# A two-layer network in fast block products: the second product in 26 block products of three slices instead of 20 of four

## Chip, core and metric

The kernel runs on one core of one Trainium2 chip. The metric is the device time of one execution in microseconds (us). The time of the kernel before is the median of three runs; one further execution was profiled.

## What is computed

```python
# x [8192 x 768] (16 x 512 rows), w1 [768 x 3072], b1 [3072], w2 [3072 x 768], all float32
y = np.matmul(x, w1) + b1
y = np.maximum(y, 0)
return np.matmul(y, w2).astype(np.float32)
```

## The kernel before, in words

**Halves and iterations.** The 3072 hidden columns are cut into two halves (c = 0 and 1), the 8192 rows into 8 blocks of 1024. The 16 iterations go through the 8 blocks with the first half of w1 and w2 resident in on-chip memory, and then through the 8 blocks with the second. In the first eight iterations the output rows are stored, in the last eight they are added to what is stored, by accumulating DMAs of GpSimd's queue (POOL).

**Fast block products.** Both products are cut into blocks and computed with fewer block products than the plain way, in the manner of Strassen: sums of blocks of the left operand are multiplied by sums of blocks of the right one, and the results are combined. Tables say how. X_SUMS and W1_SUMS give the block sums of the first product, FIRST_U and FIRST_V which sum goes into which of its 20 products, FIRST_OPS the operations that combine results; Y_SUMS, W2_SUMS, SECOND_U, SECOND_V and SECOND_OPS are the same for the second. The block sums of x and y are made anew in each iteration, on VectorE (add_x_sums, L682; add_y_sums, L908); those of w1 and w2 once for each half (L699, L723). X_FUSE and Y_FUSE name sums that are done two at once, as one instruction over two blocks ("two-wide").

**First stage of an iteration** (add_first, L917): two groups of 20 products of 6 matmuls each (L935, 128x256), 240 matmuls. The results in PSUM, TensorE's accumulator memory, are combined by ScalarE (L965, L969) and VectorE (L972, L975, L981), and the last operation of a chain adds the bias, applies the relu and writes y as float16. In iteration 0 a plain product (L845) stands in its place.

**Second stage** (add_second, L1034): 20 products, each of a 256-row by 512-column block of y (sums of y in the slots that ys gives) and a block of w2 (512 by 384). A product is 8 matmuls: four slices s of the hidden columns, summed in PSUM, times two groups j of 128 rows (L1056, 128x384).

**Chains, operations and places.** SECOND_CHAINS lists, for each of seven chains, products ('m', n) and operations ('t', n) in turn. A chain owns a pair of PSUM banks while it lasts; there are four pairs. An operation takes the pair's running result after the product ahead of it: a 'sum' is kept in on-chip memory (a place of tile s), a 'seed' is written into another chain's bank pair as that chain's start value, an 'out' is a block of the output (a place of tile o), which a DMA stores. An operation with a kept sum to add runs on VectorE (L1071), one without on ScalarE (L1068). A product that goes on in a pair waits for the operation that reads the pair before it, and the one that starts on a seed waits for the seed. So an operation lies on a loop: end of one product, operation, start of a later product on the same pair.

**Order.** SECOND_ORDER gives the order of the 20 products in an iteration. A planner in the program (Graph.run) takes all tasks with a duration each, and the order of the products as given, and writes out one fixed order for each engine; take (L300) picks places of s, o and PSUM. At run time there are only these fixed queues and semaphores between engines. SP issues the plain stores, weight loads of the second half and transposing loads of x, POOL the loads of x and the accumulating stores.

**Special iterations.** In the iterations of APART (7) the kept sum and the product's own part of an output are stored apart, the second one accumulating. In the last iteration add_priors loads the rows that the first half stored, VectorE adds them and the outputs go by plain stores; the last output is stored in two halves by two queues (L1087).

Of the kernel before, what the change touches and what calls it, by code (L numbers as in the profile page):

```python
# [9 lines left out]
FP32 = mybir.dt.float32  # L10
FP16 = mybir.dt.float16
# [19 lines left out]
X_SUMS = ((20, 4, 3, -1), (15, 4, 1, -1), (21, 7, 1, -1), (12, 0, 4, -1), (10, 5, 1, -1), (13, 0,  # L31
    6, -1), (11, 2, 6, -1), (22, 6, 7, -1), (16, 0, 1, -1), (17, 6, 1, -1), (23, 6, 3, -1), (14,
    7, 3, -1), (18, 3, 2, -1), (19, 4, 2, -1), (9, 4, 5, -1), (8, 5, 3, -1))
FIRST_U = (22, 13, 17, 8, 16, 19, 6, 14, 1, 4, 21, 18, 10, 3, 11, 9, 12, 20, 23, 15)
W1_SUMS = ((6, 2, 5, 1), (8, 6, 4, -1), (17, 1, 8, -1), (7, 0, 1, 1), (10, 8, 7, -1), (16, 3, 10,
    -1), (9, 6, 3, -1), (11, 4, 5, -1), (12, 9, 0, -1), (14, 7, 9, -1), (15, 3, 5, -1), (13, 7, 2,
    -1))
FIRST_V = (15, 0, 9, 3, 2, 0, 12, 4, 6, 17, 3, 13, 4, 16, 1, 11, 1, 10, 14, 8)
FIRST_OPS = {
    0: (0, 1, 18, 1, 'out', 0, None),  # L40
    1: (4, 1, 17, 1, 'out', 1, None),
    2: (3, 1, 19, 1, 'out', 2, None),
    3: (6, 1, 15, 1, 'out', 3, None),
    4: (7, 1, None, None, 'out', 4, (1.0, 1.0, -1.0)),
    5: (7, 1, 15, 1, 'out', 5, None),
    6: (2, 1, None, None, 'out', 6, None),
    7: (5, 1, 17, 1, 'out', 7, None),
    8: (5, 1, 19, 1, 'out', 8, None),
    9: (1, 1, 18, 1, 'out', 9, None),
    10: (6, 1, None, None, 'out', 10, (0.0, 1.0, 0.0)),  # L50
    11: (1, 1, None, None, 'out', 11, (0.0, 0.0, 1.0)),
    12: (0, 1, None, None, 'seed', 1, None),
    13: (6, 1, None, None, 'seed', 7, (-1.0, 0.0, 1.0)),
    14: (4, 1, None, None, 'seed', 5, None),
    15: (8, -1, None, None, 'sum', None, (1.0, 0.0, 0.0)),
    16: (8, -1, 20, 1, 'seed', 2, None),
    17: (8, 1, 19, 1, 'sum', None, (0.0, 1.0, -1.0)),
    18: (6, -1, 20, 1, 'sum', None, None),
    19: (0, 1, None, None, 'sum', None, (0.0, 0.0, 1.0)),
    20: (6, 1, None, None, 'sum', None, (1.0, 0.0, 0.0)),  # L60
}
FIRST_CHAINS = ((('m', 8), ('t', 19), ('m', 2), ('t', 12), ('m', 1), ('t', 0)), (('m', 10), ('t',
# [4 lines left out]
FIRST_SEEDS = (None, 12, 16, None, None, 14, None, 13, None)  # L67
FIRST_ORDER = (19, 8, 9, 24, 28, 13, 17, 4, 22, 29, 12, 3, 16, 5, 15, 33, 39, 37, 6, 32, 25, 36,
    23, 2, 18, 30, 26, 14, 1, 38, 35, 7, 10, 34, 21, 20, 27, 11, 0, 31)
SWITCH_ORDER = (19, 8, 9, 24, 28, 13, 17, 4, 22, 29, 12, 3, 16, 5, 15, 33, 39, 37, 6, 32, 25, 36,  # L70
    23, 2, 18, 30, 26, 14, 1, 38, 35, 7, 10, 34, 21, 20, 27, 11, 0, 31)

Y_SUMS = ((13, 8, 7, 1), (16, 5, 3, 1), (12, 2, 1, 1), (20, 7, 10, 1), (15, 4, 12, -1), (24, 2, 0,
    1), (19, 10, 13, 1), (23, 15, 9, -1), (26, 23, 3, -1), (14, 0, 6, -1), (17, 2, 14, 1), (18, 9,
    16, 1), (27, 14, 15, -1), (22, 17, 20, 1), (21, 18, 19, 1), (25, 11, 21, 1))
SECOND_U = (4, 11, 5, 25, 8, 13, 15, 12, 27, 19, 17, 6, 22, 24, 16, 2, 26, 18, 10, 9)
W2_SUMS = ((7, 2, 1, -1), (13, 7, 5, -1), (6, 2, 0, -1), (10, 5, 6, -1), (8, 5, 4, -1), (9, 3, 8,
    1), (12, 7, 9, -1), (15, 8, 7, -1), (11, 9, 6, -1), (14, 1, 11, 1), (16, 3, 10, 1), (17, 5, 2,
    -1))
SECOND_V = (1, 5, 6, 17, 7, 1, 11, 4, 14, 13, 12, 0, 15, 3, 0, 9, 16, 10, 4, 3)  # L80
W2_NEG = (3,)
SECOND_OPS = {
    0: (0, 1, 11, 1, 'out', 2, None),
    1: (2, 1, 9, 1, 'out', 3, None),
    2: (1, 1, 11, 1, 'out', 0, None),
    3: (2, 1, None, None, 'out', 1, None),
    4: (1, 1, 8, 1, 'out', 4, None),
    5: (3, -1, 8, 1, 'out', 5, None),
    6: (0, -1, 9, 1, 'out', 6, None),
    7: (3, 1, None, None, 'out', 7, None),  # L90
    8: (1, -1, 13, 1, 'sum', None, None),
    9: (0, 1, 10, 1, 'sum', None, None),
    10: (4, 1, 16, 1, 'sum', None, None),
    11: (5, 1, None, None, 'sum', None, None),
    12: (5, -1, None, None, 'seed', 0, None),
    13: (6, 1, None, None, 'sum', None, None),
    14: (5, 1, 16, -1, 'seed', 2, None),
    15: (1, -1, None, None, 'seed', 5, None),
    16: (1, -1, None, None, 'sum', None, None),
    17: (3, -1, 19, 1, 'seed', 1, None),  # L100
    18: (4, -1, None, None, 'seed', 3, None),
    19: (6, 1, None, None, 'sum', None, None),
}
SECOND_CHAINS = ((('m', 2), ('t', 9), ('m', 14), ('t', 0), ('m', 3), ('t', 6)), (('m', 9), ('t',
# [4 lines left out]
SECOND_SEEDS = (12, 17, 14, 18, None, 15, None)  # L109
SECOND_ORDER = (19, 5, 1, 4, 9, 18, 13, 17, 10, 15, 12, 11, 6, 7, 2, 0, 14, 8, 16, 3)  # L110
LAST_ORDER = (19, 5, 1, 4, 9, 18, 13, 17, 10, 15, 12, 11, 6, 7, 2, 0, 14, 8, 16, 3)

X_FUSE = (6, 8, 10, 12)
Y_FUSE = (5, 10, 13)
# [100 lines left out]

class Reg:
# [14 lines left out]
class Graph:  # L231
# [9 lines left out]
    def __init__(self, banks=8, sums=12, outs=4):  # L241
        self.tasks = []
        self.writer, self.readers = {}, {}
        self.npe = 0
        self.places = {"ps": [[0.0, 0] for _ in range(banks)],
                       "s": [[0.0, 0] for _ in range(sums)], "o": [[0.0, 0] for _ in range(outs)]}
# [53 lines left out]
    def take(self, reg, start, but=()):  # L300
# [22 lines left out]
        step = reg.n if reg.kind == "s" else 1  # L323
        for i in range(0, len(p) - reg.n + 1, step):
            f = max(p[k][0] for k in range(i, i + reg.n))
            if f < 1e8 and (best is None or f < best[0]):
                best = (f, list(range(i, i + reg.n)))
        return best

    def run(self, begin=0.0, lookahead=0.2, ahead=5):  # L330
# [5 lines left out]
        far = at + 50.0  # L336
# [128 lines left out]
APART = (7,)  # L465

W2_WHOLE = (4, 0)
# [3 lines left out]
class Fast:  # L471
# [6 lines left out]
    def __init__(self, nc, xf, w1, b1, w2, of):  # L478
# [8 lines left out]
        self.g = Graph()  # L487
        nw1, self.nsum = self.NCH * 12, self.NCH * 24
# [4 lines left out]
    def place_all(self):  # L493
        self.xs = place({r * 2 + k: 2 * r + k for r in range(4) for k in range(2)}, X_SUMS,
                        FIRST_U, range(8, 20))
        self.ys = place({r * 3 + h: r * 3 + h for r in range(4) for h in range(3)}, Y_SUMS,
                        SECOND_U, range(12, 20))
        self.w1s = place({k * 3 + h: 2 * h + k for k in range(2) for h in range(3)}, W1_SUMS,
                         FIRST_V, range(6, 16))
        self.w2s = [place({n * 3 + h: 2 * h + n for n in range(2) for h in range(3)}, W2_SUMS,  # L500
                          SECOND_V, range(6, 16))]
# [4 lines left out]
        self.w2s.append(place(dict(enumerate(freed[:6])), W2_SUMS, SECOND_V, freed[6:]))  # L506

    def open(self, ctx, tc):
# [9 lines left out]
        self.v2 = one.tile([P, 16, 4, self.NH], FP16, name="v2")  # L518
        self.y = one.tile([P, 20, 4 * self.QM], FP16, name="y")
        self.x = one.tile([P, 20, 3, self.QM], FP16, name="x")  # L520
        self.xn = one.tile([P, 8, self.K], FP16, name="xn")
        self.s = one.tile([P, 12, 256], FP32, name="s")
        self.o = one.tile([P, 4, self.N], FP32, name="o")
        self.ps = pool("ps", 1, space=PSUM).tile([P, 8, 512], FP32, name="ps")
        self.w1dram = dram.tile([P, self.NG, 6, 3, 2 * P], FP16, name="w1d")
        self.w2dram = dram.tile([P, 6, 4, self.NH], FP16, name="w2d")
# [3 lines left out]
    def constants(self):  # L530
        nc = self.nc
        nw1, nw2, nx, nb = self.NCH * 12, self.NCH * 12, self.M // P, self.H // P
# [32 lines left out]
    def load_w2(self, to, c, h, s):  # L565
        h0 = (12 * c + 4 * h + s) * P
        self.nc.gpsimd.dma_start(out=to[:, 2 * h:2 * h + 2, s, :],
                                 in_=self.w2[h0:h0 + P, :].rearrange("p (a n) -> p a n", a=2))
# [12 lines left out]
    def prologue(self):  # L581
        nc = self.nc
        for s in range(4):
            (nc.sync, nc.scalar)[s % 2].dma_start(out=self.o[:, s],
# [7 lines left out]
        self.load_strip(self.v1, 0, 1, 0)  # L592
# [753 lines left out]
```

## Time and profile before

| what | value |
|---|---|
| time, median of 3 runs | 865.16 us (863.69 to 865.88) |
| profiled execution, its own time | 863.6 us |
| its span (first to last instruction) | 862.1 us |
| granted clock of TensorE | 0.997 of full |
| busy: PE 850.1, DVE 699.0, ACT 475.1, POOL 125.2 us | 99, 81, 55, 15% of the span |
| moved by DMA | 117.50 MB |

PE is TensorE's matmul part, PEld its weight load, which runs beside it, DVE is VectorE, ACT ScalarE, POOL GpSimd, SP SyncE. In the rows, L1056 is line 1056 of the program; out<-in are tiles; the time in brackets is the engine's idle time ahead of the instruction and what ended it. A matmul's end is modelled: it stands until its results are through, some 0.16 us after the next matmul has begun, so that matmuls overlap in the rows, and their starts are what the pace is read from.

### The profile page before, as it was taken

The numbers are of one execution on the slowest core, as the hardware profiler recorded it, in microseconds if no ns is written. First come the engines' busy times: TensorE is split into PE (matmuls) and PEld (weight loads), VectorE is DVE, ScalarE is ACT, GpSimd is POOL, SyncE is SP. The second block draws the span as 40 slices with busy tenths as digits, with TensorE's granted clock in tenths as the row PEclk, the third lists the DMA queues.
The fourth block names the chain that finished last, engine by engine and source line by source line (L and its number), as shares of the span: only waits on it lengthen the run. The fifth ranks groups of instructions, "written<-read, shape, count | busy, mean of one in ns | idle before, by whom it ended". The sixth has DMA issues, their size and how long they took to land. (4 is left out here: it accounts for less than half of the span.)

```text
span 862.1 us, 16228 instructions
## 1 busy us (share of the span) xinstructions
PE 850.1 (99%) x6445; PEld 631.4 (73%) x6445; DVE 699.0 (81%) x1043; ACT 475.1 (55%) x945; POOL 125.2 (15%) x143
## 2 busy tenths in 40 slices
PE   8999999999999999999999999999999999999996
PEld 7568778686786868768587686867868687686873
DVE  5789887968778797887989879687786978779786
ACT  5736747566574763835658265745738336253350
POOL 5200010201001010000121303113040220402200
PEclk9999999999999999999999999999999999999998
DMA  9993494865839465480896947698786787954743
GB/s 213 198 193 100 86 258 91 162 146 93 208 74 196 113 105 156 74 220 22 277 188 85 199 69 134 121 136 130 111 127 106 121 125 124 138 89 61 128 144 129
DMA packets 161347, 117.50 MB, mean 136 GB/s; under 512 B 93148, under 2 KB 159732, under 8 KB 161012
## 3 DMA queue, kind: packets, MB, share of 16 engines
q0 software_dynamic: 48128, 56.63, 42.2%
q1 hardware_dynamic: 112672, 58.81, 27.8%
q8 instruction: 51, 0.84, 0.4%
q10 hardware_dynamic: 468, 1.00, 0.3%
q14 instruction: 28, 0.23, 0.1%
HBM read 73.94 MB, written 57.41 MB: 152 GB/s over the span
## 5 line engine op out<-in xcount | busy, mean ns | idle before, releaser
L1056 PE MATMUL ps<-v,y 128*128 128x384 f16 x2560 | 418.9, 326 | 0.1
L935 PE MATMUL ps<-x,v 128*128 128x256 f16 x3600 | 396.1, 273 | 0.9 <-DVE o L1071 0.5
L935 PEld LDWEIGHTS <-v 128*128 128x128 f16 x3600 | 352.2, 98 | 44.0 <-issue 1.7
L1056 PEld LDWEIGHTS <-y 128*128 128x128 f16 x2560 | 250.5, 98 | 164.5 <-issue 0.6
L972 DVE CUSTOM_DVE_ANT_0 y<-ps,s 128x512 f16<-128x512 f32 x240 | 161.4, 688 | 63.5 <-PE ps L935 45.7
L908 DVE TENSOR_TENSOR y<-y 128x1024 f16<-128x1024 f16 (+2 forms) x227 | 165.5, 754 | 4.9 <-ACT y L854 2.2
L969 ACT ACTIVATE s<-ps,bt 128x256 f32<-128x256 f32 x180 | 73.9, 472 | 115.7 <-PE ps L935 114.2
L682 DVE TENSOR_TENSOR x<-x 128x768 f16<-128x768 f16 (+1 forms) x168 | 109.7, 684 | 0.5
L1101 POOL DMA_DIRECT2D out_dram<-o x62 | 74.4, 1275 | 178.2 <-DMA out_dram<-s 60.8
L1068 ACT ACTIVATE ps<-ps 128x768 f32<-128x768 f32 x48 | 38.2, 795 | 110.0 <-PE ps L1056 94.2
L579 POOL DMA_DIRECT2D xn<-in_x_dram x30 | 22.9, 763 | 491.1 <-ACT xn L641 352.4
L1068 ACT ACTIVATE s<-ps 128x768 f32<-128x768 f32 x64 | 51.8, 811 | 61.0 <-PE ps L1056 60.1
L969 ACT ACTIVATE y<-ps,bt 128x256 f16<-128x256 f32 x180 | 73.5, 472 | 15.7 <-PE ps L935 13.9
L1071 DVE TENSOR_TENSOR o<-ps,s 128x768 f32<-128x768 f32 x56 | 52.9, 954 | 8.9 <-PE ps L1056 4.7
L641 ACT ACTIVATE xn<-xn 128x768 f16<-128x768 f16 x64 | 53.5, 838 | 3.9 <-DMA x<-xn 2.5
L1071 DVE TENSOR_TENSOR s<-ps,s 128x768 f32<-128x768 f32 x32 | 30.6, 956 | 11.4 <-PE ps L1056 11.1
L981 DVE TENSOR_TENSOR s<-s,ps 128x512 f32<-128x512 f32 x30 | 20.5, 684 | 19.0 <-PE ps L935 19.0
L969 ACT ACTIVATE ps<-ps,bt 128x256 f32<-128x256 f32 x60 | 26.9, 448 | 16.3 <-PE ps L935 8.7
L1068 ACT ACTIVATE o<-ps 128x768 f32<-128x768 f32 x36 | 29.0, 809 | 12.1 <-PE ps L1056 12.0
L965 ACT ACTIVATE ps<-ps 128x512 f32<-128x512 f32 x60 | 34.9, 582 | 0.9 <-DVE y L972 0.2
L845 PE MATMUL ps<-x,v 128*128 128x256 f16 (+1 forms) x216 | 31.9, 308 | 0.9 <-DMA v<-in_w_dram 0.6
L1071 DVE TENSOR_TENSOR o<-s,ps 128x768 f32<-128x768 f32 x28 | 26.6, 949 | 7.2 <-DMA out_dram<-o 6.1
(61 smaller groups left out, 353.7 us busy)
## 6 DMA issues: line engine op xcount, KB each, us to landing
out_dram<-o SPq DMA_DIRECT2D x65, 384.0 KB, 6.4
out_dram<-o POOLq DMA_DIRECT2D x62, 384.0 KB, 6.9
xn<-in_x_dram POOLq DMA_DIRECT2D x28, 768.0 KB, 8.3
x<-out_dram SPq DMA_DIRECT2D x8, 384.0 KB, 3.3
v<-in_w_dram POOLq DMA_DIRECT2D x6, 384.0 KB, 9.1
v<-in_w_dram POOLq DMA_DIRECT2D x12, 192.0 KB, 10.0
w1d<-in_w_dram POOLq DMA_DIRECT2D x6, 384.0 KB, 15.8
w2d<-in_w_dram POOLq DMA_DIRECT2D x12, 192.0 KB, 13.7
```

What stands on the lines that cost most here:

```text
L641: self.nc.scalar.activation(out=self.xn[:, s, :], in_=self.xn[:, s, :], func=ACTF.Square, accum_out=self.stat[:, self.stat_at["x"] + i:][: ...
L682: self.nc.vector.tensor_tensor(out=self.two(x, out), in0=self.two(x, in0), in1=self.two(x, in1), op=ALU.add if sign > 0 else ALU.subtract)
L845: nc.tensor.matmul(self.ps[:, ps.at[0], cols], lhsT=self.v1[:, gi, 2 * h + k2, k, j * P:(j + 1) * P], rhs=rhs, start=(k2 == 0 and k == 0), ...
L908: self.nc.vector.tensor_tensor(out=self.two(y, out), in0=self.two(y, in0), in1=self.two(y, in1), op=ALU.add if sign > 0 else ALU.subtract)
L935: nc.tensor.matmul(self.ps[:, at, j * self.QM:(j + 1) * self.QM], lhsT=self.v1[:, gi, self.w1s[FIRST_V[p]], k, j * P:(j + 1) * P], rhs=sel ...
L965: nc.scalar.activation(out=out, in_=ps, scale=float(a), func=func if kind == "out" else ACTF.Copy)
L969: nc.scalar.activation(out=out[:, halves[j]], in_=ps[:, halves[j]], func=func, scale=float(a), bias=beta(j))
L972: nc.vector._custom_dve(TENSOR_ADD_SAT, out=out, in0=ps, in1=s, s0=F_MAX, s1=0.0)
L1056: nc.tensor.matmul(self.ps[:, bank[ch].at[j], 0:NH], lhsT=self.y[:, self.ys[SECOND_U[p]], m0:m0 + P], rhs=self.v2[:, slot[SECOND_V[p]], s, :],
L1068: nc.scalar.activation(out=out, in_=ps, func=ACTF.Copy, scale=float(a))
L1071: engine.tensor_tensor(out=out, in0=in0, in1=in1, op=ALU.add if a == b else ALU.subtract)
L1101: nc.gpsimd.dma_start(out=rows, in_=out, accum_op=ALU.add)
```

## The change

The second product is cut another way. A block of y has 256 rows and 384 hidden columns (three slices h, was four slices s), a block of w2 384 by 384. A 4 by 4 arrangement of y blocks times a 4 by 2 arrangement of w2 blocks takes 26 products of 6 matmuls (was a 4 by 3 times 3 by 2 arrangement in 20 products of 8). With it come:

- 28 sums of y blocks (was 16), 18 of w2 blocks (was 12), new chains (eight), operations (26) and order. Five pairs of y sums are two-wide (was three), two of x (was four).
- y has 23 slots of 768, fewer than the 16 blocks and 28 sums. A new function, place_between, puts a sum into the slot of one that is no longer needed, and says after which product that may be. add_y_sums is called ahead of every product and adds the sums whose slot the product before has freed; before, all sums stood ahead of the first product.
- Kept sums and outputs share one tile s of eight places, each of 768 float32; before they had s (12 places of 256) and o (four of 768). An operation that uses a kept sum for the last time writes over it.
- The first product's tables are new as well (again 20 products in two groups); its outputs go to two y slots each.
- Output operation 6 (SPLIT) stores its kept sum and its product's part apart in every iteration, 7 and 8 are the iterations that do so for all (APART, was 7).
- In the last iteration only the outputs of LAST_DIRECT take loaded priors; the others are accumulated by POOL.
- w1 sums are made for each group alone (was both at once), w2 sums whole (1152 elements). All six loads of w1 stand ahead of those of w2 at the start; for the second half w1 is loaded in 12 DMAs (was 2), w2 in 8 (was 6).

The core of the diff:

```diff
-SECOND_ORDER = (19, 5, 1, 4, 9, 18, 13, 17, 10, 15, 12, 11, 6, 7, 2, 0, 14, 8, 16, 3)
+SECOND_CHAINS = ((('m', 5), ('t', 2)), (('m', 24), ('t', 0)), (('m', 13), ('t', 24), ('m', 4),
+    ('t', 23), ('m', 12), ('t', 18), ('m', 1), ('t', 17), ('m', 23), ('t', 9), ('m', 16), ('t',
+    4), ('m', 9), ('t', 5)), (('m', 10), ('t', 22), ('m', 18), ('t', 20), ('m', 0), ('t', 15),
+    ('m', 14), ('t', 6)), (('m', 17), ('t', 21), ('m', 8), ('t', 19), ('m', 3), ('t', 16), ('m',
+    19), ('t', 14), ('m', 7), ('t', 8), ('m', 6), ('t', 3), ('m', 20), ('t', 1)), (('m', 2), ('t',
+    13), ('m', 21), ('t', 12), ('m', 25), ('t', 7)), (('m', 11), ('t', 11), ('m', 22), ('t', 10)),
+    (('m', 15), ('t', 25)))
+SECOND_SEEDS = (8, 10, None, 23, 24, 18, 13, None)
+SECOND_ORDER = (13, 15, 4, 17, 10, 8, 18, 12, 3, 0, 1, 2, 14, 23, 19, 21, 11, 25, 7, 16, 22, 5, 6,
+    9, 24, 20)
+LAST_DIRECT = (0, 1, 2, 3, 5)
-X_FUSE = (6, 8, 10, 12)
-Y_FUSE = (5, 10, 13)
+X_FUSE = (0, 2)
+Y_FUSE = (7, 9, 13, 18, 26)
+S_SLOTS, Y_SLOTS = 8, 23
...
+def place_between(order, sums, used, raw, slots, fused):
+    slot, live, free = {n: n for n in range(raw)}, set(range(raw)), list(range(raw, slots))
+    last = {used[p]: n for n, p in enumerate(order)}
+    since, at = [], -1
+    for n, (o, _, _, _) in enumerate(sums):
+        later = {v for s in sums[n + 1:] for v in s[1:3]}
+        old = sorted(live - later, key=lambda v: (last.get(v, -1), v))
+        for v in old:
+            if v not in last:
+                live.discard(v)
+                free.append(slot[v])
+        if not free:
+            v = [v for v in old if v in last][0]
+            at = max(at, last[v])
+            live.discard(v)
+            free.append(slot[v])
+        slot[o] = free.pop(0)
+        live.add(o)
+        since.append(at)
...
-APART = (7,)
+SPLIT = (6,)
+APART = (7, 8)
...
-    def add_y_sums(self, groups=(0, 1)):
+    def add_y_sums(self, order, done):
+        n, since = 0, self.y_from[order]
+        for out, in0, in1, sign in self.sums_of(Y_SUMS, self.ys[order], Y_FUSE):
+            at, n = n, n + len(out)
+            if since[at] != done - 1:
+                continue
...
-            sj = [(s, j) for s in range(4) for j in range(2)]
+            hj = [(h, j) for h in range(3) for j in range(2)]
...
-                                 lhsT=self.y[:, self.ys[SECOND_U[p]], m0:m0 + P],
-                                 rhs=self.v2[:, slot[SECOND_V[p]], s, :],
-                                 start=(start and s == 0), stop=(s == 3), skip_group_check=True)
+                                 lhsT=self.y[:, ys[SECOND_U[p]], m0:m0 + P],
+                                 rhs=self.v2[:, slot[SECOND_V[p]], h, :],
+                                 start=(start and h == 0), stop=(h == 2), skip_group_check=True)
...
             if kind == "m":
+                self.add_y_sums(order, done)
+                done += 1
...
                 if what == "sum":
-                    dest = kept[n] = Reg("s", 3)
+                    dest = kept[n] = Reg("s") if u is None or u in uses else kept[u]
```

More of the change, by code (lines that the diff above doesn't have):

```diff
@@ L68 @@
[L68 to L75, printed above, removed]
@@ L213, in place @@
     return slot
+def place_between(order, sums, used, raw, slots, fused):
[17 more added lines that the diff above has]
+        since.append(at)
+    for n in fused:
+        since[n] = since[n + 1]
+    made = {s[0]: since[n] for n, s in enumerate(sums)}
+    for n, p in enumerate(order):
+        assert made.get(used[p], -1) < n, p
+    return slot, since
 class Reg:
@@ L763, in add_stats @@
                 for i in range(6) if first and (i in FIRST_V) == kept]
-        todo += [lambda i=i: self.add_stat_w2(c, i, after) for i in range(6)
+        todo += [lambda i=i: self.add_stat_w2(c, i, after) for i in range(8)
                  if second and (i in SECOND_V) == kept]
@@ L1037, in add_second @@
         final = it == self.NIT - 1
-        apart = it in APART
+        apart = {t for t in SECOND_OPS if (t in SPLIT or it in APART)
+                 and SECOND_OPS[t][2] is not None and not (final and t in LAST_DIRECT)}
         order = LAST_ORDER if final else SECOND_ORDER
-        slot = self.w2s[c]
-        bank, kept = {}, {}
+        slot, ys = self.w2s[c], self.ys[order]
+        bank, kept, done = {}, {}, 0
+        uses = [SECOND_OPS[t][2] for t in SECOND_OPS]
         NH, QM = self.NH, self.QM
@@ L1076, in operation @@
             ps = pair(bank[ch])
[L1077 to L1087 removed]
+            out = pair(dest) if kind == "seed" else sum_of(dest)
+            if kind == "out" and final and t in LAST_DIRECT:
+                if t in folds:
+                    combine(nc.scalar, out, ps, a, None, None)
                 else:
@@ L1118, in add_second @@
                     bank[ch] = Reg("ps", 2, leaves=1)
-                u, w = self.ys[SECOND_U[n]], slot[SECOND_V[n]]
-                self.g.add("PE", 1301, lambda p=n, ch=ch, start=start: product(p, ch, start),
-                           reads=self.y_keys(u, 0) + self.y_keys(u, 1) +
-                           [("w2", w, s) for s in range(4)] + ([] if start else [bank[ch]]),
-                           writes=[bank[ch]])
+                t = SECOND_CHAINS[ch][-1][1]
+                if final and t in LAST_FOLD and t in LAST_DIRECT and not start and SECOND_CHAINS[ch][-2] == ("m", n):
+                    fold(t)
+                    folds.add(t)
+                u, w = ys[SECOND_U[n]], slot[SECOND_V[n]]
+                self.g.add("PE", 976, lambda p=n, ch=ch, start=start: product(p, ch, start),
+                           reads=self.y_keys(u) + [("w2", w, h) for h in range(3)] +
+                           ([] if start else [bank[ch]]), writes=[bank[ch]])
                 continue
@@ L1205, in plan @@
         self.presets()
-        self.hold = [g.held(Reg("o"), [s]) for s in range(4)]
+        self.hold = [g.held(Reg("s"), [s]) for s in range(4)]
         self.first_block()
```

469 lines of the change are left out of this document (252 added, 217 removed), and 16 rows, old and new, of tables (FIRST_CHAINS, SECOND_CHAINS, Y_SUMS).

## The prediction

> **What bounds the kernel now.** I read the page's busy times first, then the waits of TensorE, then two stages in the middle of the run, then single instructions at their edges. Columns of the first rows: busy us (share), instructions; below, the groups have busy us, mean ns of one | idle before.
>
> ```profile
> span 862.1 us, 16228 instructions
> PE 850.1 (99%) x6445; PEld 631.4 (73%) x6445; DVE 699.0 (81%) x1043; ACT 475.1 (55%) x945; POOL 125.2 (15%) x143
> ...
> L1056 PE MATMUL ps<-v,y 128*128 128x384 f16 x2560 | 418.9, 326 | 0.1
> L935 PE MATMUL ps<-x,v 128*128 128x256 f16 x3600 | 396.1, 273 | 0.9 <-DVE o L1071 0.5
> ```
>
> TensorE is busy for 99% of the span, and 815 us of that are two lines. The list of TensorE's waits has only single short ones; its longest and its only one on a result of the second product:
>
> ```profile
> PE ps L601 <- DVE ones L542: 1.3, 1, 1.3
> ...
> PE ps L935 <- DVE o L1071: 0.5, 1, 0.5
> ```
>
> One second stage (304.25 to 330.25) and the first stage behind it, with busy time of each engine, granted clock, DMA share and GB/s:
>
> ```profile
> 304.25:330.25 26.00, 26.00 (x162) 15.65 (x160) 23.64 (x31) 12.48 (x23) 2.88 (x4) 1.00 0.76 162
> 330.25:356.45 26.20, 26.20 (x242) 23.48 (x240) 18.55 (x30) 16.05 (x38) 0.00 (x0) 1.00 0.43 97
> sum 52.20, PE 52.20 PEld 39.14 DVE 42.19 ACT 28.53 POOL 2.88; mean PE 26.10 PEld 19.57 DVE 21.10 ACT 14.27 POOL 1.44
> ```
>
> TensorE fills both stages at the full clock. VectorE has 10 of 52.2 us free, so TensorE's stream sets the time, and it stays so only while every eviction comes back before TensorE needs the bank pair. How near that is, single instructions show (start, length, engine, line):
>
> ```profile
> 304.25 13.00 PE L1056 MATMUL ps<-v,y 128*128 128x384 f16 x79
> ...
> 305.75 0.80 ACT L1068 ACTIVATE ps<-ps 128x768 f32<-128x768 f32 x1 [0.29 <-PE ps L1056]
> ...
> 308.42 0.96 DVE L1071 TENSOR_TENSOR ps<-s,ps 128x768 f32<-128x768 f32 x1 [0.34 <-PE ps L1056]
> ...
> 310.95 0.81 ACT L1068 ACTIVATE s<-ps 128x768 f32<-128x768 f32 x1 [0.49 <-PE ps L1056]
> ...
> 313.61 0.80 ACT L1068 ACTIVATE ps<-ps 128x768 f32<-128x768 f32 x1 [0.32 <-PE ps L1056]
> ```
>
> 79 matmuls in 13.00 us, the last one 0.326 long, make a start-to-start of (13.00 - 0.326)/78 = 0.1625 us, and 1.30 for a product of eight. Products begin at 304.25 + 1.30 n, so their boundaries are 305.55, 308.15, 310.75, 313.35. ScalarE starts 0.20 us after its boundary (305.75, 310.95), or 0.26 (313.61) where in the program it also waits for an instruction of its own engine; VectorE starts 0.27 after (308.42). The way back, where it is late:
>
> ```profile
> 204.69 5.08 PE L1056 MATMUL ps<-v,y 128*128 128x384 f16 x29
> ...
> 205.79 1.49 ACT L1068 ACTIVATE s<-ps 128x768 f32<-128x768 f32 x2
> ...
> 207.33 2.21 PEld L1056 LDWEIGHTS <-y 128*128 128x128 f16 x14 [0.27 <-issue]
> ```
>
> ScalarE ends at 207.28, TensorE takes up its weights at 207.33: 0.05 back. The 29 matmuls should take 28 x 0.1625 + 0.326 = 4.88 and take 5.08: 0.20 us was lost, and the list of waits has none of it. So a late eviction stalls TensorE without an idle row, because a matmul's modelled end (0.326) runs 0.16 past the next start.
>
> **What it removes.** The second stage goes from 20 products of 8 matmuls to 26 of 6, per iteration 160 to 156, over 16 iterations 2560 to 2496; the first product keeps 3600. 64 x 0.1625 = **-10.4 us**. The matmuls keep their 384 columns and the clock is 1.00, so the price is sound.
>
> **What the shorter product adds.** A product is now 6 x 0.1625 = 0.975 us. With one product between a bank's last matmul and its reuse, a turn through ScalarE takes 0.20 to 0.26 + 0.80 to 0.81 + 0.05 = 1.05 to 1.12. Before, 1.30 covered that, and VectorE's 0.27 + 0.96 + 0.05 = 1.28 too. Now 0.975 doesn't cover it: TensorE stands for 0.07 to 0.15. Turns through VectorE have two products (1.95) or more between in the new order, so they are covered. By SECOND_CHAINS and SECOND_ORDER and the order of the built instructions, four turns of an iteration go through ScalarE with one product between and aren't behind another stall: product 13 to 4 (operation 24), 4 to 10 or 17 to 8, which share a stall (23, 21), 10 to 18 (22), and 21 to 25 (12). Two of them wait for an instruction of ScalarE's own as well. At 0.07 each it is 0.29 an iteration, 4.6 us in 16; at 0.15 each 0.59, 9.5 us. Two at 0.13 to 0.15 and two at 0.07 to 0.13 give about 0.44: **+7.0 us**.
>
> **Places that occur once.** At these, instructions queued before an eviction take longer than TensorE's products between. Their prices, and the turn of VectorE's second products, are these groups (busy us, mean ns):
>
> ```profile
> L972 DVE CUSTOM_DVE_ANT_0 y<-ps,s 128x512 f16<-128x512 f32 x240 | 161.4, 688 | 63.5 <-PE ps L935 45.7 <-ACT s L969 14.3
> ...
> L908 DVE TENSOR_TENSOR y<-y 128x1024 f16<-128x1024 f16 x150 | 99.8, 686 | 1.6
> ...
> L908 DVE TENSOR_TENSOR y<-y 128x2048 f16<-128x2048 f16 x45 | 54.9, 1221 | 0.8
> ...
> L682 DVE TENSOR_TENSOR x<-x 128x768 f16<-128x768 f16 x112 | 60.1, 550 | 0.2
> ...
> L682 DVE TENSOR_TENSOR x<-x 128x1536 f16<-128x1536 f16 x56 | 52.6, 951 | 0.3
> ...
> L1068 ACT ACTIVATE s<-ps 128x768 f32<-128x768 f32 x64 | 51.8, 811 | 61.0 <-PE ps L1056 60.1
> ...
> L975 DVE SCALAR_TENSOR_TENSOR s<-ps,bt,s 128x256 f32<-128x256 f32 x60 | 26.2, 477 | 3.8 <-PE ps L935 3.8
> ...
> L908 DVE TENSOR_TENSOR y<-y 128x512 f16<-128x512 f16 x32 | 12.6, 420 | 2.5 <-ACT y L854 2.2
> ...
> L708 ACT ACTIVATE v<-v 128x1536 f16<-128x1536 f16 x2 | 2.9, 1470 | 0.0
> ...
> 848.98 2.69 DVE L1109 TENSOR_TENSOR x<-x,s 128x768 f32<-128x768 f32 x3
> ```
>
> Three of 0.95 in a row take 2.69, so VectorE starts the next 0.08 before the end of the last. In iteration 1 a chain of three L972, two L975 and one x sum stands in one turn of the first product: 0.27 + 3 x 0.69 + 2 x 0.48 + 0.55 - 5 x 0.08 + 0.05 = 3.5 against four products of 6 x 0.109 (26.20/240) = 2.6: 0.8. In iteration 8, where the w2 signs stand ahead of operation 12 on ScalarE (now 128x1152, so 1.1 to 1.47), 0.7 and 0.2; VectorE at the same change of halves 1.3 in four places; in the last iteration 0.25. Together 3.3, partly on the same products. The first second product waits for eight w2 sums and two y sums behind the last w2 load; by 0.55 to 0.95 each that is level with TensorE's own work there or up to 0.8 over. **+2.5 us**, bounds 1.5 and 3.5.
>
> **The tail.** The last rows of the run before:
>
> ```profile
> 828.22 26.16 PE L1056 MATMUL ps<-v,y 128*128 128x384 f16 x160
> ...
> 853.68 1.82 DVE L1071 TENSOR_TENSOR o<-ps,x 128x768 f32<-128x768 f32 x2
> ...
> 855.42 1.01 DVE L1071 TENSOR_TENSOR o<-x,ps 128x384 f32<-128x384 f32 x2
> ```
>
> The last boundary is 828.22 + 160 x 0.1625 = 854.22; the two halves start 1.20 later, behind two whole outputs queued on VectorE. After, one output stands ahead, and it is done about 0.3 after the boundary: **-0.8 us**, between -1.1 and -0.3.
>
> **What I cost at nothing.** VectorE: y sums go from 150 of 128x1024, 45 of 2048 and 32 of 512 to 288 of 768 and 80 of twice 768: 288 x 0.55 + 80 x 0.95 = 234 for 167 us. x sums 168 x 0.55 + 28 x 0.95 = 119 for 113; w1 and w2 sums 5 more; operations of the second product some 30 fewer of 0.95. The first product's outputs go into two slots of y as two runs of 256 and no longer as one of 512; two-wide sums already go over two slots and show no price for it (0.951, under 2 x 0.550). In all 699 + 67 + 6 + 5 - 28 = 749 at most, 87%: still not the bound, and TensorE covers it. The added wait is that y sums now lie between products, four of an iteration waiting for TensorE to give up a slot of y. Behind each are x sums and evictions; the freed slots come from products 0 to 4 of 26, and in the new order no turn behind them is longer than TensorE's work between, but for the places counted. Where that cover goes is the third case below. ScalarE: 251 operations for 148, 103 x 0.81 = 83 more, 559 of 860: covered. Stores:
>
> ```profile
> out_dram<-o SPq DMA_DIRECT2D x65, 384.0 KB, 6.4
> out_dram<-o POOLq DMA_DIRECT2D x62, 384.0 KB, 6.9
> ```
>
> POOL's accumulating stores go from 62 to 87, SP's stores fall by two: 23 x 0.39 = 9 MB more beside the DMA's 0.76 and 0.43 shares. Landing takes 6.4 and 6.9 us; only four slots of s are now rewritten within 7.5 us of TensorE's work, where 16 were in s and o before, so sharing the slots costs nothing unless landings pass 9 (66 then, for 47). SP issues 12 loads of w1 for 2 at the change of halves and 8 of w2 for 6, and three priors fewer at the end; each issue holds SP's queue alone, with iterations to spare. In the last iteration operations 4, 6 and 7 accumulate through POOL: operation 4 has seven products (6.8 us) behind it, so 6.9 of landing ends before the last store does.
>
> **The sum.** -10.4 + 7.0 + 2.5 - 0.8 = -1.7 against the profiled execution's 863.6 us (span 862.1 and 1.5 around it): 861.9. That execution lies 1.6 under the median of the three runs, 865.16, so the median comes to **863.5**. With all terms at their ends: -5.4 to +2.3, **859.8 to 867.5**.
>
> **Rivals.** *The turnaround stays hidden.* If the next matmul can be taken up while the eviction still runs, or the four turns start earlier than 0.20, nothing of the 7.0 is paid: -8.7, median 856.5. For it: the list of waits shows no stall on ScalarE. Against it: the 5.08 us at 204.69. I give it 0.22.
>
> *VectorE's evictions come late: slower.* At its tightest, in some three turns of a first stage, a bank is reused two products (1.31 us) after its last matmul; an L972 eviction needs 0.27 + 0.69 + 0.05 = 1.01, so 0.30 is left. One sum of 0.55 in front delays it by 0.55 - 0.27 = 0.28 and just fits; a two-wide sum (0.95 - 0.08 - 0.27 = 0.60) or two sums in a row make it 0.30 to 0.45 late. In the built order a first stage holds 13 sums of x and y where it held 5, and VectorE's free time there falls from 7.65 to about 3.5 us. In the second stage 1.95 - 1.28 leaves 0.67, and a two-wide sum fits. Two late evictions an iteration are 2 x 0.30 x 16 = 9.6: median 873.1; all three would be 877.9. It decides from one an iteration (4.8, 868.3). For it: L972 already waited only 0.26 us a piece before (63.5/240), so little margin is shown. Against it: no more turns are that tight than before, and in the new order no two sums stand in front of one. 0.26.
>
> The Trainium skill speaks for this rival: "VectorE: DVE Perf Modes", section The DRAIN you can't avoid, says that the next VectorE operation doesn't start until the pipe is empty. By it no 0.08 would be saved between neighbours, and VectorE would have 1177 x 0.08 = 94 us more to do, 843 of 860. The trace doesn't bear it out here: three of 0.95 in 2.69.
>
> That the change doesn't do what it says is excluded: the 2496 matmuls are counted in the built program.
>
> **How the numbers follow.** The forecast has 0.52: of it 0.18 under 862.6, 0.32 in the band, 0.02 above. A measurement of this kernel can tell 0.3%, 2.6 us, from no change: the band is 862.6 to 867.8. Faster 0.18 + 0.22 = 0.40, same 0.32, slower 0.02 + 0.26 = 0.28. The likeliest case's own range is 859.8 to 867.5; 855.5 to 874.0 also takes in most of the hidden case and the first half of the late one, and leaves some 0.18 out.
>
> **What would show it.** Right: second-stage products 0.975 apart with four gaps an iteration of 0.07 to 0.15 between matmuls, each ending 0.05 after a ScalarE operation; halves at the end 0.3 after the boundary; VectorE at 740 to 750. Wrong: no such gaps (856.5), or first-stage gaps that end after L1023 evictions with two sums ahead of them (873), or waits on stores of s.

## The result, and the profile after

The changed kernel takes 876.85 us (median of 4 runs, 874.74 to 878.86) against 864.83 for the kernel before (4 runs): a ratio of 1.0139, 95% interval 1.0107 to 1.0171. It is slower by 1.4%; the forecast was 863.5, and the range ended at 874.0. The profiled execution spans 877.3 us.

The page of the profile after, the rows that answer to those of before (busy us and share; groups with busy us, mean ns | idle before; DMA issues with us to landing):

```profile
span 877.3 us, 16551 instructions
...
PE 852.7 (97%) x6381; PEld 624.9 (71%) x6381; DVE 755.1 (86%) x1207; ACT 556.5 (63%) x1066; POOL 154.5 (18%) x168
...
L1109 PE MATMUL ps<-v,y 128*128 128x384 f16 x2496 | 417.5, 326 | 4.8 <-ACT s L1120 4.0
L980 PE MATMUL ps<-x,v 128*128 128x256 f16 x3600 | 399.7, 273 | 9.7 <-DVE ps L1031 5.8
...
out_dram<-s POOLq DMA_DIRECT2D x87, 384.0 KB, 8.4
out_dram<-s SPq DMA_DIRECT2D x68, 384.0 KB, 6.6
```

ScalarE has the work that was reckoned (557 us for 559); VectorE has 755, 6 more than the 749 that were given as its most. What is new is idle time ahead of the first product's matmuls, 9.7 us for 0.9, and accumulating stores that land after 8.4 us where they took 6.9. The lists of waits of TensorE and of ScalarE (us in total, times, longest):

```profile
PE ps L980 <- DVE ps L1031: 5.8, 12, 0.9
PE ps L1109 <- ACT s L1120: 4.0, 2, 3.7
```

```profile
ACT s L1020 <- DMA out_dram<-s: 23.9, 23, 2.6
...
ACT s L1120 <- DMA out_dram<-s: 7.4, 4, 4.0
```

ScalarE waits 31 us for stores of s. In the kernel before it waits for none on its kept sums; there VectorE waits 8.6 us for places of o, and TensorE loses 4.9 us in all (table below). One such wait in a first stage, in order of time (start, length, engine, line):

```profile
133.15 0.84 ACT L1020 ACTIVATE s<-ps,bt 128x256 f32<-128x256 f32 x2 [1.01 <-DMA out_dram<-s]
...
134.02 0.69 DVE L1023 CUSTOM_DVE_ANT_0 y<-ps,s 128x512 f16<-128x512 f32 x1 [1.49 <-ACT s L1020]
134.35 0.85 ACT L783 ACTIVATE junk<-junk 128x768 f16<-128x768 f16 x1
134.63 0.55 DVE L735 TENSOR_TENSOR x<-x 128x768 f16<-128x768 f16 x1
...
135.09 0.69 DVE L1031 TENSOR_TENSOR ps<-s,ps 128x512 f32<-128x512 f32 x1
...
135.83 1.36 PE L980 MATMUL ps<-x,v 128*128 128x256 f16 x11 [0.69 <-DVE ps L1031]
```

ScalarE may not write its kept sum (L1020) until a store has read the place. VectorE's L1023 needs that sum and starts 1.49 us late. L1031 stands behind it and behind one x sum (L735, 0.55 us), and TensorE stands behind L1031. The list of waits names L1031; what came late was a store.

Since a late eviction shows as idle time only in part, I add up what the starts of neighbouring matmuls lie apart beyond the usual for their shape (gaps of over 0.03 us), by stage. The change of halves is iteration 8's second stage and the first stage behind it:

| us lost, profiled execution | before second stage 0 | second stages | iteration 7's second, 8's first | change of halves | iteration 1's first stage | other first stages | all |
|---|---|---|---|---|---|---|---|
| before | 2.7 | 0.2 | 0.2 | 0.9 | 0.0 | 0.9 | 4.9 |
| after | 3.1 | 7.0 | 1.3 | 10.6 | 1.1 | 8.2 | 31.3 |

26.4 more are lost, 10.4 saved by 64 fewer matmuls, 0.7 at the tail (below): 15.3, and the spans differ by 15.2.

### The profile page after: what moved, and what is told of

Same layout as the page of the kernel before. It is cut to its first block, busy times and chain, and to the rows that moved or that the text cites. A ratio compares the mean times of both kernels' runs of the same rounds, so it can differ in the third digit from the quotient of the medians.

```text
span 877.3 us, 16551 instructions
## 1 busy us (share of the span) xinstructions
PE 852.7 (97%) x6381; PEld 624.9 (71%) x6381; DVE 755.1 (86%) x1207; ACT 556.5 (63%) x1066; POOL 154.5 (18%) x168
## 5 line engine op out<-in xcount | busy, mean ns | idle before, releaser
L980 PEld LDWEIGHTS <-v 128*128 128x128 f16 x3600 | 352.3, 98 | 56.3 <-issue 14.1
L1109 PEld LDWEIGHTS <-y 128*128 128x128 f16 x2496 | 243.5, 98 | 174.3 <-issue 16.1
L953 DVE TENSOR_TENSOR y<-y 128x768 f16<-128x768 f16 (+1 forms) x368 | 225.4, 641 | 10.4 <-ACT y L899 0.2
L1023 DVE CUSTOM_DVE_ANT_0 y<-ps,s 128x512 f16<-128x512 f32 x240 | 159.2, 687 | 60.4 <-ACT s L1020 36.2
L1120 ACT ACTIVATE s<-ps 128x768 f32<-128x768 f32 x171 | 138.4, 810 | 93.4 <-PE ps L1109 80.4
L1020 ACT ACTIVATE s<-ps,bt 128x256 f32<-128x256 f32 x180 | 75.3, 472 | 80.7 <-PE ps L980 55.8
L735 DVE TENSOR_TENSOR x<-x 128x768 f16<-128x768 f16 (+1 forms) x196 | 113.4, 607 | 1.3 <-DVE x L735 1.0
L1158 POOL DMA_DIRECT2D out_dram<-s x73 | 88.0, 1412 | 145.8 <-ACT s L1120 90.6
L1120 ACT ACTIVATE ps<-ps 128x768 f32<-128x768 f32 x80 | 63.6, 795 | 47.2 <-DVE s L1126 32.7
L1126 DVE TENSOR_TENSOR s<-ps,s 128x768 f32<-128x768 f32 x85 | 80.6, 957 | 5.9 <-PE ps L1109 3.2
L1020 ACT ACTIVATE y<-ps,bt 128x256 f16<-128x256 f32 x180 | 72.0, 474 | 16.3 <-PE ps L980 16.3
L1126 DVE TENSOR_TENSOR s<-s,ps 128x768 f32<-128x768 f32 x59 | 56.2, 952 | 8.5 <-PE ps L1109 8.0
L1020 ACT ACTIVATE ps<-ps,bt 128x256 f32<-128x256 f32 x60 | 26.7, 448 | 28.1 <-PE ps L980 26.9
L1161 POOL DMA_DIRECT2D out_dram<-s x14 | 17.1, 1300 | 126.4 <-ACT s L1120 126.4
L1026 DVE SCALAR_TENSOR_TENSOR s<-ps,bt,s 128x256 f32<-128x256 f32 x60 | 26.2, 478 | 5.1 <-PE ps L980 3.0
L890 PEld LDWEIGHTS <-v 128*128 128x128 f16 x216 | 20.9, 98 | 11.4 <-DMA v<-in_w_dram 0.9
```

Of the source, the lines that this page charges most:

```text
L735: self.nc.vector.tensor_tensor(out=self.two(x, out), in0=self.two(x, in0), in1=self.two(x, in1), op=ALU.add if sign > 0 else ALU.subtract)
L890: nc.tensor.matmul(self.ps[:, ps.at[0], cols], lhsT=self.v1[:, gi, 2 * h + k2, k, j * P:(j + 1) * P], rhs=rhs, start=(k2 == 0 and k == 0), ...
L953: self.nc.vector.tensor_tensor(out=self.two(self.y, out), in0=self.two(self.y, in0), in1=self.two(self.y, in1), op=ALU.add if sign > 0 els ...
L980: nc.tensor.matmul(self.ps[:, at, j * self.QM:(j + 1) * self.QM], lhsT=self.v1[:, gi, self.w1s[c][gi][FIRST_V[p]], k, j * P:(j + 1) * P], ...
L1020: nc.scalar.activation(out=out[:, j], in_=ps[:, j], func=func, scale=float(a), bias=beta(j))
L1023: nc.vector._custom_dve(TENSOR_ADD_SAT, out=out, in0=ps, in1=s, s0=F_MAX, s1=0.0)
```

## Experiments

In each group of runs the kernel before was run on the same chip; its median there was 863.5 to 864.1, and 864.83 beside the changed kernel. The four runs of the changed kernel lie 4.1 us apart, so a difference to its median is good to a microsecond or two; where it matters I also give the difference that comes out when each kernel is set against the kernel before of its own group. Lost times by stage are worked out as above, from one profiled execution each.

**Thin stores.** Is it the places, held until a store has landed?

```diff
-                nc.gpsimd.dma_start(out=rows, in_=out, accum_op=ALU.add)
+                n = 64 if c else NH
+                nc.gpsimd.dma_start(out=rows[:, :, 0:n], in_=out[:, :, 0:n], accum_op=ALU.add)
```

(and the same in store_sum).

> The changed kernel, but the accumulating stores of the second half (iterations 8 to 14, and the accumulating ones of 15) move 64 of each 384 columns; the rest of the output is left at what the first half stored. Order and instructions stay the same, only a slot of s is held for a shorter time. Theory (s slots held by stores that land late): the 9.3 us lost around 490 to 513 us and about 3.3 us of first-stage gaps behind it go, the first half keeps its own; 876.9 - 12 = 865, between 863 and 868. Rival (VectorE's added sums make the evictions late): the same gaps stay, 876 to 878.

Measured: 863.19 us (10 runs), ratio to before 0.9993, interval 0.9983 to 1.0003: 13.7 us under the changed kernel (12.7 against the kernels before). The change of halves falls from 10.6 to 1.5, the first stages behind it from 4.5 to 0.7 us; the first half, whose plain stores are whole, keeps 2.4 of 3.7. Its stores of L1159 (L1158 in the changed kernel) and its rows beside the 23.9 and 5.8 of above, from the line's view and the two lists of waits (landing in us, then us in total, times, longest):

```profile
DMA to landing us min/median/max: 2.9/3.4/11.3
```

```profile
ACT s L1020 <- DMA out_dram<-s: 5.6, 7, 1.3
...
PE ps L980 <- DVE ps L1031: 1.8, 4, 0.8
```

All 1207 VectorE instructions are still there, in the same order. The rival, that they alone make the evictions late, falls.

**The kernel before with the same thin stores.**

> The kernel before with the same thin accumulating stores in its second half. Theory (before, outputs had slots of their own and no eviction on the path waited for a store): no change, 864 to 866. Rival (less traffic helps whatever the slots are): 2 to 4 us faster, 861 to 863.

Measured: 863.15 us, ratio 0.9990, interval 0.9981 to 1.0000. At most 0.2%, 1.6 us: less traffic alone does not make what the thin stores bring in the changed kernel.

**Evictions by bank.** Does ScalarE's turn cost what was forecast? (banks is true for operations 12, 21, 22, 23 and 24.)

```diff
-            if final and p == order[-1]:
-                hj.sort(key=lambda q: q[1])
+            hj.sort(key=lambda q: q[1])
...
+                if engine is nc.scalar and banks:
+                    for j in range(2):
+                        nc.scalar.activation(out=out[:, j], in_=ps[:, j], func=ACTF.Copy,
+                                             scale=float(a))
```

> The changed kernel, with the six matmuls of every second product sorted by bank and operations 12, 21, 22, 23 and 24 done by ScalarE as two instructions of one bank each. The first can start three matmuls before the product's end, the second is done 0.8 us after it, under the 0.975 of one product. Theory (ScalarE's turn is longer than a product, 0.49 us an iteration): -7.6 us, 869.3, between 868 and 871. Rival (the stores' holds absorb it, since a faster TensorE only meets them earlier): -2 or less, 875 to 877. Each second instruction costs ScalarE some 0.1 us, which neither counts.

Measured: 869.89 us, ratio to before 1.0079 (1.0062 to 1.0096): 7.0 under the changed kernel (6.0 against the kernels before). The second stages lose 0.3 instead of 7.0 us. The same second stage in both kernels, first as changed, then by bank (windows; the first column is the stage):

```profile
307.99:333.87 25.88, 25.88 (x159) 15.28 (x158) 24.16 (x35) 17.68 (x29) 3.90 (x5) 1.00 0.80 134
```

```profile
304.79:330.14 25.35, 25.35 (x159) 15.26 (x157) 23.88 (x35) 17.88 (x34) 3.90 (x5) 1.00 0.77 134
```

By bank it is 156 x 0.1625 = 25.35 us, with nothing lost; 0.5 us less, and busy time is 100% in both. In the changed kernel only the weight loads and ScalarE's rows show where the 0.5 went:

```profile
309.26 0.80 ACT L1120 ACTIVATE ps<-ps 128x768 f32<-128x768 f32 x1 [0.18 <-ACT y L1020]
...
311.33 0.80 ACT L1120 ACTIVATE ps<-ps 128x768 f32<-128x768 f32 x1 [0.34 <-PE ps L1109]
```

```profile
310.10 1.88 PEld L1109 LDWEIGHTS <-y 128*128 128x128 f16 x12 [0.18 <-issue]
312.18 1.88 PEld L1109 LDWEIGHTS <-y 128*128 128x128 f16 x12 [0.20 <-issue]
314.27 0.74 PEld L1109 LDWEIGHTS <-y 128*128 128x128 f16 x5 [0.21 <-issue]
```

309.26 + 0.80 = 310.06, and the weights go on at 310.10; 312.13 and 312.18. That is the 0.05 back of the prediction.

**Both at once.**

> Both at once: thin accumulating stores in the second half (64 of each 384 columns; the rest of the output keeps the first half's values) and the evictions by bank. Theory (two separate losses): 863.2 - 7.0 = 856.2, between 855 and 858. Rival (one loss hides part of the other): 859 or more.

Measured: 857.06 us, ratio 0.9920 (0.9903 to 0.9936). 863.19 - 7.0 = 856.2 was expected. Beside the thin stores the eviction by bank brings 6.1 us, without them 6.0 to 7.0: within the spread of the runs the two losses add up.

**Iteration 8 stored once.**

```diff
-APART = (7, 8)
+APART = (7,)
```

> The changed kernel with APART = (7,): iteration 8 stores each output once, as the others do, and eight of its operations go back to VectorE. Theory (two accumulating stores to the same rows, one behind the other, held the slots at the change of halves): most of the 9.3 us there goes, 0 to 3 us come back as VectorE's work ahead of evictions: 868 to 873. Rival (the change of halves is short of VectorE's time, and that is why the outputs were stored apart): no faster, 876 to 882.

Measured: 873.59 us, ratio 1.0115 (1.0098 to 1.0132): 3.3 us under the changed kernel, just outside what the theory gave, and not clear of the spread, since the intervals of the two ratios overlap. The change of halves loses 8.7 instead of 10.6, and the list of TensorE's waits names another engine:

```profile
PE ps L980 <- DVE x L735: 4.4, 3, 3.9
```

```profile
495.70 2.95 DVE L735 TENSOR_TENSOR x<-x 128x768 f16<-128x768 f16 x5
```

These five x sums on VectorE stand ahead of a product there, and operations that the doubled stores had spared VectorE are its own again. Between 459 and 498 us no eviction of this run waits for a store; in the changed kernel ScalarE's evictions wait 6.3 us for them there. So both theories hold a part: storing once ends the waits for stores at this place, and what is lost there then goes through VectorE.

**Nine places, and its control.** Are there too few places, with all stores whole? A ninth place is added, and the planner is told that a store lands after 8.0 us and not 6.5.

```diff
-S_SLOTS, Y_SLOTS = 8, 23
+S_SLOTS, Y_SLOTS = 9, 23
...
-                           lat=9.0 if it == 0 else 3.5 if direct else 6.5)
+                           lat=9.0 if it == 0 else 3.5 if direct else 8.0)
...
+FP8 = mybir.dt.uint8
...
-        self.junk = self.const.tile([P, self.K], FP16, name="junk")
+        self.junk = self.const.tile([P, self.K], FP8, name="junk")
```

(evictions by bank in both; the control has the memory edits alone).

> Evictions by bank, nine places in s instead of eight, and a planner that reckons with 8.0 us for a store's landing instead of 6.5. The ninth place's memory comes from the guard on the inputs' ranges: its comparison is left out, its squares are still made but written as bytes and summed into 32 columns. All stores are whole. Theory (too few places for the stores' landing time): of 869.9, the first-stage gaps (about 9.5 us) and most of the change of halves' (3.4) go: 857 to 861, under the kernel before. Rival (the gaps are VectorE's, and the thin stores only gave the DMA queues room): 867 to 871.

> Control for the nine places: the same without the guard's comparison, with evictions by bank, but eight places and 6.5 us in the planner. Both theories: as the evictions by bank alone, 868 to 870; at most 1.2 us less, the one gap that ends with the guard's flag.

Measured: 866.37 us with nine (ratio 1.0044, 1.0029 to 1.0058), 870.76 with eight (1.0080, 1.0062 to 1.0098). The gain is 4.4 us by the medians, 3.1 by the ratios, and not 9 to 13: the expectation for the size fails. Where it came, it is as the theory has it. "Other first stages" lose 0.8 us for 5.7, while L1154's stores (L1158 of the changed kernel) land as late as ever:

```profile
DMA to landing us min/median/max: 5.0/8.2/15.8
```

So those gaps go though no store lands sooner: what was short there is a place. Nine places with the planner's old 6.5 us were not run, so the ninth place and an order that reckons with 8.0 us are shown together; 8.0 us alone is the next run. The change of halves keeps 8.2 of 9.8. There ScalarE's evictions follow the stores:

```profile
486.76 0.81 ACT L1116 ACTIVATE s<-ps 128x768 f32<-128x768 f32 x1 [2.98 <-DMA out_dram<-s]
488.73 0.81 ACT L1116 ACTIVATE s<-ps 128x768 f32<-128x768 f32 x1 [1.16 <-DMA out_dram<-s]
490.65 0.81 ACT L1116 ACTIVATE s<-ps 128x768 f32<-128x768 f32 x1 [1.11 <-DMA out_dram<-s]
492.60 0.84 ACT L1013 ACTIVATE s<-ps,bt 128x256 f32<-128x256 f32 x2 [1.14 <-DMA out_dram<-s]
494.53 0.84 ACT L1013 ACTIVATE s<-ps,bt 128x256 f32<-128x256 f32 x2 [1.08 <-DMA out_dram<-s]
```

One place comes free each 1.94 us ((494.53 - 486.76)/4): 393 KB in that time are 203 GB/s, and all DMA together moves as much there (windows of this run; the last column is GB/s):

```profile
488.00:495.00 7.00, 4.07 (x36) 3.30 (x35) 1.92 (x4) 2.93 (x6) 5.05 (x5) 0.99 1.17 203
```

On these figures the stores make up nearly all the traffic there, and one lands at a time. Why they come no faster is not shown; a slice of the changed kernel's page has 268 GB/s. Iteration 8 has 15 accumulating stores, 29 us of such traffic for a stage of 25.4.

**The planner told the true time.** Eight places, evictions by bank, lat 8.0 for 6.5.

> Evictions by bank, eight places, only the planner's landing time 8.0 instead of 6.5 us. If the order were what is wrong, a planner with the true time should get most of it back: 860 to 864. Theory (eight places are too few for any order of these chains): no more than 4 us either way, 866 to 874.

Measured: 885.22 us, ratio 1.0235 (1.0211 to 1.0258), 15 us slower than by bank alone, outside both. Told the truer time, the planner finds a worse order for eight places, so its landing time is not what was wrong by itself. Whether some other order for eight places does better is not shown.

**Fewer doubled stores at the change of halves.** With nine places and evictions by bank, the operations that iteration 8 stores apart are: none, operations 0, 3 and 7, or 4 and 7, or 4, 5 and 7 (operation 6 always).

```diff
-        apart = {t for t in SECOND_OPS if (t in SPLIT or it in APART)
+        apart = {t for t in SECOND_OPS if (t in SPLIT or it == 7 or (it == 8 and t in (4, 7)))
```

> Nine places, evictions by bank, landing 8.0 us in the planner, the guard's comparison left out as in the nine places before; and APART = (7,): iteration 8 stores each output once. TensorE's first matmuls take their ones from a place of s, as GpSimd's matrix for it came late (0.5 us). Theory (at the change of halves 15 accumulating stores of 384 KB go through at one per 1.92 us, 29 us for a stage of 25): with nine stores the DMA has room, but VectorE gets its eight operations back beside the w2 sums and x sums, which stood for 6.5 us in the same change with eight places: 862 to 866. Rival (places were all that was short there): 858 to 860.

> As the run before, but in iteration 8 operations 0, 3 and 7 (and 6, as always) store their two parts apart, the rest once: 12 accumulating stores, 23 us at 1.92 us each, inside the stage, and three operations fewer on VectorE than with none. Theory (DMA rate against VectorE's time at the change of halves): the 8.2 us lost there fall to 2 to 5, 860 to 863, below the kernel before (863.8). Rival (either of the two is the bound whatever the split): 865 to 867.

> As the run with operations 0, 3 and 7 apart in iteration 8, but apart are the two outputs that are done first, 4 and 7 (and 6). Theory (what the first stage behind the change of halves waits for is a place held by the last accumulating stores): with the doubled stores early and 11 in all, they are through before the first stage starts, and its 5.8 us fall to 1 to 3: 859 to 862. Rival (VectorE's x sums behind late outputs are what it waits for): 864 to 866, since the late outputs go through VectorE now.

> The same with 4, 5 and 7 apart: 12 stores as in the run with 0, 3 and 7, only earlier. Theory: 859 to 862, as the run with 4 and 7 or up to 1 us better, for one operation less on VectorE. Rival: 864 to 866.

| apart in iteration 8 | us | ratio to before, 95% | lost at the change of halves, us |
|---|---|---|---|
| none | 864.94 | 1.0011 (1.0002 to 1.0021) | 7.8 |
| 0, 3, 7 | 864.26 | 1.0001 (0.9990 to 1.0012) | 6.3 |
| 4, 7 | 861.83 | 0.9979 (0.9969 to 0.9989) | 5.1 |
| 4, 5, 7 | 864.25 | 1.0008 (0.9999 to 1.0017) | 7.6 |

With none and with 4 and 7 the time is in the theory's range, with 0, 3 and 7 between theory and rival, with 4, 5 and 7 in the rival's. The version with 4 and 7 is the only one with whole stores that beats the kernel before, by 0.2%, and it leaves out the guard's comparison.

The change of halves does not fall to the 2 to 5 us that were expected, nor, with 4 and 7, the first stage behind it to 1 to 3 (it loses 4.6). In all four TensorE's longest wait there, 3.0 to 4.3 us, is for x sums on VectorE. With the 12 stores of 0, 3, 7 and of 4, 5, 7 ScalarE's evictions also wait some 4 us for stores between 459 and 498 us. With none and with 4 and 7 they wait for no store there, and VectorE has hardly a free moment; with 4 and 7 (TensorE's wait, and the window ahead of its end, in which VectorE is busy 27.22 of 28.30 us):

```profile
PE ps L975 <- DVE x L730: 4.7, 3, 3.0
```

```profile
463.50:491.80 28.30, 25.29 (x167) 15.95 (x164) 27.22 (x43) 17.88 (x33) 14.83 (x13) 0.99 0.96 160
```

So the stores alone do not account for this place: without their waits VectorE's time is lost there. How the loss of the versions with 12 and 15 stores divides between the two stays open.

## Why the prediction was wrong

**The removed matmuls** were right: 25.35 us for 156 matmuls, where the evictions go by bank.

**ScalarE's turn** was right in place and size. In the changed kernel's undisturbed second stages, that of iteration 5 for one, the matmuls' starts lie further apart at four places, ahead of products 4, 10, 18 and 25, by 0.12, 0.13, 0.15 and 0.09 us. Those are the four turns that were named, 0.49 us an iteration for 0.44. 7.0 was forecast, the second stages outside the change of halves and iteration 7 lose 7.0, and the eviction by bank gives back 6.0 to 7.0. The case in which it stays hidden is refuted.

**Places that occur once** came out in the range. With the stores thin, 1.1 us are lost in iteration 1, 1.3 around iteration 7 and 1.5 at the change of halves, 3.9, and the kernel before lost 1.1 at the same places: 2.8 more, 2.5 forecast. About 1.0 of that is ScalarE's turn in the two second stages among them, so 1.8 is this term's own, inside its bounds of 1.5 and 3.5. The single places were forecast less well: in iteration 1 the loss is 0.2, 0.45 and 0.4 ahead of three products, not 0.8 ahead of one (the sum there, 3.5 against 2.6, makes 0.9).

**The tail** was right. The last rows of TensorE and VectorE and the last store:

```profile
867.73 2.51 PE L1109 MATMUL ps<-v,y 128*128 128x384 f16 x13
...
869.23 1.89 DVE L1126 TENSOR_TENSOR s<-ps,x 128x768 f32<-128x768 f32 x3 [0.18 <-PE ps L1109]
...
871.18 0.39 SPq L1151 DMA_DIRECT2D out_dram<-s  x1
```

The last boundary is 867.73 + 2.51 - 0.16 = 870.08. VectorE is through 1.0 us after it, at 871.12; before it was 2.2 (855.42 + 1.01 - 854.22). 7.2 us follow the boundary to the end of the span; before, 862.1 - 854.22 = 7.9. So 0.7 for 0.8.

**The step that failed** is under "What I cost at nothing": "so sharing the slots costs nothing unless landings pass 9". It was the right condition with the wrong landing. I took 6.4 and 6.9 us, the medians of before, for a kernel that issues 25 more accumulating stores; they land at 8.4 in the median and 16.4 at most (those of L1161), 38 of the 87 after more than 9 us, where 2 of 62 did before; and my own count had 66 reuses within 9 us. I also passed over APART = (7, 8): iteration 8 doubles its accumulating stores, and I never set 15 of them against one stage. This step was put at 0 and cost 12.7 to 13.7 us by the thin stores in the second half, besides about 3 us in the first half, which goes with nine places (5.7 to 0.8 over both halves). At the change of halves it is bound up with VectorE's time, as the runs with fewer doubled stores show.

With thin stores the time comes near the forecast, 863.19 for 863.5, and that is in part luck. The forecast stood 1.7 us under a kernel before of 865.16; the run is 0.7 under one of 863.88, and some 2 us of waits in the first half are still in it.

**The rival that was slower** had the sign and nearly the size (873.1), but another cause. VectorE's evictions in the first stage do come late, and now and then a sum stands ahead of one, as in the rows at 134.63; but what makes them late is that the kept sum that they read had no place yet. With every sum still in its place and the stores thin, these gaps fall from 4.5 to 0.7 us in the second half. "Waits on stores of s" stood in the last part as a sign that the forecast is wrong, with no chance and no price of its own. The section of the Trainium skill that the prediction quotes for this rival, The DRAIN you can't avoid in "VectorE: DVE Perf Modes", goes on to say that a next operation that is not held starts earlier; the 0.08 us of the rows agree with that part, so the section does not speak for the rival as plainly as the prediction has it.

## To carry to other kernels

When results and intermediates begin to share places, price the longest hold first: count the places, the stores in one stage, and the landing time that the new traffic will have, not the old median. A stall that a trace puts on VectorE may begin at a DMA two steps back; follow the releasers before believing in compute. When a product becomes shorter, every eviction that was just covered by one product must be looked at again, and splitting it by bank with the matmuls sorted so can hide it: here it cost ScalarE 0.2 us a stage (17.88 for 17.68).

## What the runs showed of the hardware

After a long stall TensorE can go on at half speed. In the changed kernel (the stall ends at 494.52; the column after the busy times is the granted clock):

```profile
490.50:494.52 4.02, 0.36 (x3) 0.10 (x1) 2.88 (x6) 0.81 (x1) 0.09 (x1) 0.92 1.16 202
494.52:497.03 2.51, 2.51 (x9) 1.28 (x9) 0.00 (x0) 0.81 (x1) 0.00 (x0) 0.50 1.16 202
```

Nine matmuls take 2.51 us. So one long stall costs more than itself, here 1.3 us (half of the 2.51), and in the run with iteration 8 stored once 2.5 more (clock 0.50 for 4.9 us).

The length of the gap does not decide it alone. From start to start of the matmuls, the half clock follows gaps of 3.3 to 4.6 us in eight of the kernels, but also one of 2.70 (nine places) and ones of 2.11 and 2.73 (the planner told 8.0 us), and it does not follow one of 2.25 (nine places) or one of 3.54 (evictions by bank). What sorts them is a fixed step: in each trace the granted clock changes only at times that lie whole multiples of 3.41 us apart. In the run with the planner's 8.0 us, the first two lines, and with evictions by bank, the last three (columns: PE, PEld, DVE, ACT, POOL, clock, DMA share, GB/s):

```profile
440.11:443.52 3.41, 1.57 (x14) 1.13 (x12) 3.41 (x8) 1.56 (x4) 0.00 (x0) 1.00 1.15 192
443.52:446.94 3.42, 3.42 (x18) 2.36 (x17) 2.04 (x4) 1.43 (x3) 0.00 (x0) 0.50 0.43 76
```

```profile
484.28:487.69 3.41, 2.02 (x13) 1.08 (x12) 3.41 (x6) 0.80 (x1) 1.54 (x2) 1.00 1.15 203
487.69:491.10 3.41, 1.59 (x12) 1.14 (x12) 1.23 (x3) 1.34 (x2) 0.00 (x0) 1.00 1.17 203
491.10:494.51 3.41, 2.17 (x20) 1.79 (x19) 0.00 (x0) 1.14 (x3) 1.52 (x2) 1.00 1.17 203
```

In all the traces, from the first second stage to the last, each step at full clock in which TensorE is busy for 1.57 us or less is followed by one at half clock, 12 in all, and none with 1.59 or more is. The gap of 3.54 us lay across two steps. No run varied the gap on purpose, so the bound is an observation of these traces. The Trainium skill ("TensorE: Matmul & The Clock Gate", section What's actually happening) has the clock fall back after an idle window of about 3.4 us that runs freely. The step of 3.41 us agrees with it; that the window is idle throughout does not, since a step that was busy for 1.57 of its 3.41 us was enough here.
